# Grouped instance normalisation: VectorE alone normalises, with a shorter chain of statistics, fixed slots and half the instructions on VectorE and ScalarE

## The chip, the cores and the metric

One core of one Trainium2 chip. The metric is the device time of the whole program in microseconds (us), lower is better; most executions agree within 0.3%. With one core there is no second die to compare with; every run that is used here, unless the text says otherwise, was of the fast state, and the granted clock was 1.0 in all of them.

## The reference

```python
# x: (4, 8, 16, 256, 256) fp32, 134 MB;  gamma: (8, 16) fp32
mu  = x.mean(axis=(3, 4), keepdims=True)
var = ((x - mu) ** 2).mean(axis=(3, 4), keepdims=True)
out = (x - mu) / np.sqrt(var + 1e-5) * gamma[None, :, :, None, None]
```

512 channels of 65,536 numbers are each normalised on their own. All data is read once and written once: 134.2 MB in, 134.2 MB out.

## The kernel before

A unit is 16 channels, 128 partitions by 8,192 columns, 4 MB; there are 32 units and six buffers. All loads are issued by SyncE, all stores by ScalarE. A load waits until the store that empties its buffer has landed.

```python
    for u in range(6):
        load(u)                                   # nc.sync.dma_start, 4 MB each
    nc.scalar.dma_start(out=g_row[:], in_=gv[None, :])
    # ... gamma is spread to columns here, at the start: copy, 8 matmuls, copy

    def coefficients(u):                          # SQ = 4096
        nc.vector.reduce_sum(out=sums[:, j : j + 1], in_=t[:, a:b], axis=AX.X)
        for c in range(a, b, SQ):
            nc.scalar.activation(out=junk[:], in_=t[:, c : c + SQ], func=ACTF.Square,
                                 accum_out=sqs[:, n : n + 1])
        nc.vector.reduce_sum(out=mv[:, 0:1], in_=sums[:], axis=AX.X)
        nc.vector.reduce_sum(out=mv[:, 1:2], in_=sqs[:], axis=AX.X)
        nc.tensor.matmul(out=ps[:], lhsT=avg..., rhs=mv[:], start=True, stop=True)
        # then on VectorE: copy from PSUM, negate, variance; root on ScalarE;
        # reciprocal, times gamma, shift on VectorE
        ...
    for u in range(U):
        scale, shift = coefficients(u)
        norm_vector(t, 0, DV, scale, shift)       # DV = 5376 of 8192 columns
        norm_scalar(t, DV, F, scale, shift)       # the other 2816, on ScalarE
        nc.scalar.dma_start(out=ov[u], in_=t[:])
        if u + 6 < U:
            load(u + 6)
```

Of the kernel before, what the change touches and what calls it, by code (L numbers as in the profile page):

```python
# [6 lines left out]

F32 = mybir.dt.float32
BF16 = mybir.dt.bfloat16
ALU = mybir.AluOpType  # L10
ACTF = mybir.ActivationFunctionType
AX = mybir.AxisListType


@with_exitstack
def kernel(
    ctx: ExitStack,
    tc: tile.TileContext,
    x: bass.AP,
    gamma: bass.AP,  # L20
    out: bass.AP,
):
    nc = tc.nc
    B, G, C, H, W = x.shape
    P = nc.NUM_PARTITIONS
    HW = H * W
    n_ch = B * G * C
    S = 8
    K = P // S
    F = HW // S  # L30
    U = n_ch // K
    NG = (G * C) // K
    SQ = 4096
    DV = 5376
    assert HW % S == 0 and (G * C) % K == 0 and F % SQ == 0

    xv = x.rearrange("b g c h w -> (b g c h w)").rearrange("(u p f) -> u p f", p=P, f=F)
    ov = out.rearrange("b g c h w -> (b g c h w)").rearrange("(u p f) -> u p f", p=P, f=F)
    gv = gamma.rearrange("g c -> (g c)")

    data = ctx.enter_context(tc.tile_pool(name="data", bufs=6))
    singles = ctx.enter_context(tc.tile_pool(name="singles", bufs=1))
    stats_pool = ctx.enter_context(tc.tile_pool(name="stats", bufs=2))
    psum = ctx.enter_context(tc.tile_pool(name="psum", bufs=2, space=bass.MemoryType.PSUM))
    ctx.enter_context(tc.manual_schedule())

    def spans(widths):
        edges = [0]
        for w in widths:
            edges.append(edges[-1] + w)  # L50
        assert edges[-1] == F
        return list(zip(edges[:-1], edges[1:]))

    load_spans, store_spans = {}, {}
    whole = spans([F])

    tiles = {}

    def load(u):
        t = data.tile([P, F], F32, name="xt")  # L60
        for a, b in load_spans.get(u, whole):
            nc.sync.dma_start(out=t[:, a:b], in_=xv[u, :, a:b])
        tiles[u] = t

    for u in range(6):
        load(u)


    g_row = singles.tile([1, G * C], F32, name="g_row")
    nc.scalar.dma_start(out=g_row[:], in_=gv[None, :])  # L70
    eps_t = singles.tile([P, 1], F32, name="eps_t")
    nc.vector.memset(eps_t[:], 1e-5)
    avg = singles.tile([P, K, S], F32, name="avg")
    nc.gpsimd.memset(avg[:], 1.0 / HW)
    nc.gpsimd.affine_select(
        out=avg[:], in_=avg[:], pattern=[[-S, K], [0, S]], compare_op=ALU.is_ge,
        fill=0.0, base=0, channel_multiplier=1,
    )
    nc.gpsimd.affine_select(
        out=avg[:], in_=avg[:], pattern=[[S, K], [0, S]], compare_op=ALU.is_ge,  # L80
        fill=0.0, base=S - 1, channel_multiplier=-1,
    )
    one = singles.tile([1, 1], F32, name="one")
    nc.vector.memset(one[:], 1.0)
    g_rep = singles.tile([1, NG, K, S], F32, name="g_rep")
    nc.vector.tensor_copy(  # L86
        out=g_rep[:],
        in_=g_row[:].rearrange("o (n k) -> o n k", n=NG).unsqueeze(3).to_broadcast([1, NG, K, S]),
    )
    g_ps = psum.tile([P, NG], F32, name="g_ps", bufs=1)  # L90
    for n in range(NG):
        nc.tensor.matmul(  # L92
            out=g_ps[:, n : n + 1],
            lhsT=g_rep[:, n].rearrange("o k s -> o (k s)"),
            rhs=one[:],
            start=True, stop=True,
        )
    g_col = singles.tile([P, NG], F32, name="g_col")
    nc.vector.tensor_copy(out=g_col[:], in_=g_ps[:])  # L99

    junk = singles.tile([P, SQ], BF16, name="junk")

    def coefficients(u):
        t = tiles[u]
        sums = stats_pool.tile([P, len(load_spans.get(u, whole))], F32, name="sums")
        sqs = stats_pool.tile([P, F // SQ], F32, name="sqs")
        n = 0
        for j, (a, b) in enumerate(load_spans.get(u, whole)):
            nc.vector.reduce_sum(out=sums[:, j : j + 1], in_=t[:, a:b], axis=AX.X)  # L109
            for c in range(a, b, SQ):  # L110
                nc.scalar.activation(  # L111
                    out=junk[:], in_=t[:, c : c + SQ], func=ACTF.Square,
                    accum_out=sqs[:, n : n + 1],
                )
                n += 1
        mv = stats_pool.tile([P, 2], F32, name="mv")
        nc.vector.reduce_sum(out=mv[:, 0:1], in_=sums[:], axis=AX.X)  # L117
        nc.vector.reduce_sum(out=mv[:, 1:2], in_=sqs[:], axis=AX.X)  # L118
        ps = psum.tile([P, 2], F32, name="ps")
        nc.tensor.matmul(  # L120
            out=ps[:], lhsT=avg[:].rearrange("p k s -> p (k s)"), rhs=mv[:],
            start=True, stop=True,
        )
        cm = stats_pool.tile([P, 2], F32, name="cm")
        nc.vector.tensor_copy(out=cm[:], in_=ps[:])  # L125
        nmean = stats_pool.tile([P, 1], F32, name="nmean")
        nc.vector.tensor_scalar(  # L127
            out=nmean[:], in0=cm[:, 0:1], scalar1=-1.0, scalar2=None, op0=ALU.mult,
        )
        var = stats_pool.tile([P, 1], F32, name="var")  # L130
        nc.vector.scalar_tensor_tensor(  # L131
            out=var[:], in0=cm[:, 0:1], scalar=nmean[:], in1=cm[:, 1:2],
            op0=ALU.mult, op1=ALU.add,
        )
        std = stats_pool.tile([P, 1], F32, name="std")
        nc.scalar.activation(out=std[:], in_=var[:], func=ACTF.Sqrt, bias=eps_t[:], scale=1.0)  # L136
        rstd = stats_pool.tile([P, 1], F32, name="rstd")
        nc.vector.reciprocal(out=rstd[:], in_=std[:])  # L138
        scale = stats_pool.tile([P, 1], F32, name="scale")
        g = u % NG  # L140
        nc.vector.tensor_mul(out=scale[:], in0=rstd[:], in1=g_col[:, g : g + 1])  # L141
        shift = stats_pool.tile([P, 1], F32, name="shift")
        nc.vector.tensor_mul(out=shift[:], in0=nmean[:], in1=scale[:])  # L143
        return scale, shift

    def norm_vector(t, a, b, scale, shift):
        nc.vector.tensor_scalar(  # L147
            out=t[:, a:b], in0=t[:, a:b], scalar1=scale[:], scalar2=shift[:],
            op0=ALU.mult, op1=ALU.add,
        )  # L150

    def norm_scalar(t, a, b, scale, shift):
        nc.scalar.activation(  # L153
            out=t[:, a:b], in_=t[:, a:b], func=ACTF.Identity, bias=shift[:], scale=scale[:],
        )

    for u in range(U):
        scale, shift = coefficients(u)
        t = tiles.pop(u)
        if u in store_spans:  # L160
            for j, (a, b) in enumerate(store_spans[u]):
                (norm_scalar if j == 1 else norm_vector)(t, a, b, scale, shift)
            for a, b in store_spans[u]:
                nc.scalar.dma_start(out=ov[u, :, a:b], in_=t[:, a:b])
        else:
            norm_vector(t, 0, DV, scale, shift)
            norm_scalar(t, DV, F, scale, shift)
            nc.scalar.dma_start(out=ov[u], in_=t[:])
        if u + 6 < U:
            load(u + 6)  # L170


# [28 lines left out]
```

## Time and profile before

Before: 628.93 us (median of 3 runs, 628.9 to 629.06).

| | before |
|---|---|
| span of the profiled run | 627.1 us |
| moved | 268.5 MB at a mean of 428 GB/s |
| VectorE / ScalarE busy | 66% / 54% |
| a unit on the DMA engines | about 19.4 us for 4 MB in and 4 MB out |
| instructions in the profile | 937 |

From the page of the kernel before: the busy row of VectorE (DVE) and the DMA share in tenths over 40 equal slices of the span, the rate in each slice, and the DMA queues with their packets, megabytes and share of the 16 engines' time.

```profile
span 627.1 us, 937 instructions
...
DVE  2999657766577665686656866558665577655770
...
DMA  8999999999999999999999999999999999999997
GB/s 368 435 403 433 435 435 435 433 435 435 435 433 435 435 435 431 433 428 433 435 427 435 431 435 433 433 433 435 435 433 435 435 435 435 433 433 435 435 433 314
...
q1 hardware_dynamic: 4608, 134.22, 49.9%
q10 hardware_dynamic: 4610, 134.22, 49.6%
q14 instruction: 6, 0.05, 0.0%
...
```

The DMA engines are busy in all slices, at 427 to 435 GB/s nearly everywhere. Moving 268.4 MB at 435 GB/s takes 617.1 us, so only some 10 us of the span are open to any change. (The Trainium skill, "DMA: Bandwidth & Descriptors", Specifications, gives 435 GB/s as the ceiling of the fabric; the slices agree.)

The groups that matter, from the page of the kernel before (columns: line, engine, operation, out<-in, shapes, count, busy us, mean ns of one, then idle time before it and what ended it), and the DMA issues (KB, median us from issue to landing).

```profile
...
L109 DVE TENSOR_REDUCE sums<-xt 128x1 f32<-128x8192 f32 x32 | 277.9, 8686 | 150.4 <-DMA xt<-in_x_dram 150.4
...
L147 DVE TENSOR_SCALAR xt<-xt,scale,shift 128x5376 f32<-128x5376 f32 x32 | 98.5, 3079 | 1.2
L153 ACT ACTIVATE xt<-xt,shift,scale 128x2816 f32<-128x2816 f32 x32 | 87.5, 2734 | 22.0 <-DVE shift L143 22.0
...
out_dram<-xt ACTq DMA_DIRECT2D x32, 4096.0 KB, 41.3
...
```

VectorE's reduce waits 150 us in all for loads: the compute has slack in the middle of the run. Stores land 41 us after their issue, though 4 MB alone take under 10 us: both queues are several transfers deep.

The first store and the last unit, from the timeline of the kernel before (columns: start us, us, engine, line, operation).

```profile
...
27.46 0.38 ACTq L168 DMA_DIRECT2D out_dram<-xt  x1
...
```

```profile
...
598.43 8.69 DVE L109 TENSOR_REDUCE sums<-xt 128x1 f32<-128x8192 f32 x1 [5.13 <-DMA xt<-in_x_dram]
...
609.59 3.08 DVE L147 TENSOR_SCALAR xt<-xt,scale,shift 128x5376 f32<-128x5376 f32 x1
...
612.76 0.34 ACTq L168 DMA_DIRECT2D out_dram<-xt  x1
```

The first store is issued at 27.46. The last load has landed at 598.43; the last store is issued at 612.76, 14.33 us later. The tail, from a table of stretches (the last two columns are the share of the DMA engines and GB/s):

```profile
...
core 0: us, PE busy (x) PEld busy (x) DVE busy (x) ACT busy (x) POOL busy (x), PEclk, DMA share, GB/s
...
613.00:614.00 1.00, 0.00 (x0) 0.00 (x0) 0.00 (x0) 0.00 (x0) 0.00 (x0) 1.00 1.22 524
614.00:622.00 8.00, 0.00 (x0) 0.00 (x0) 0.00 (x0) 0.00 (x0) 0.00 (x0) 1.00 0.93 401
622.00:623.00 1.00, 0.00 (x0) 0.00 (x0) 0.00 (x0) 0.00 (x0) 0.00 (x0) 1.00 1.14 492
623.00:624.00 1.00, 0.00 (x0) 0.00 (x0) 0.00 (x0) 0.00 (x0) 0.00 (x0) 1.00 0.16 66
624.00:625.00 1.00, 0.00 (x0) 0.00 (x0) 0.00 (x0) 0.00 (x0) 0.00 (x0) 1.00 0.15 66
...
```

A finer table of the same stretch also has this line:

```profile
...
615.00:616.00 1.00, 0.00 (x0) 0.00 (x0) 0.00 (x0) 0.00 (x0) 0.00 (x0) 1.00 0.53 229
...
```

### The profile page before, as it was taken

What the parts mean: (1) busy time and instruction counts of PE and PEld (TensorE: products, weight loads), DVE (VectorE), ACT (ScalarE), POOL (GpSimd) and SP (SyncE); (2) the same over time, 40 slices, a digit from 0 to 9 for tenths busy, and PEclk for the clock granted to TensorE, in tenths of its full rate; (3) what the DMA queues carried; (4) which work ended last, traced back from release to release, by engine and by line L of the source; (5) the groups of instructions that cost most, each with busy time, mean ns of one, the idle gap of its engine ahead of it and who ended that gap; (6) DMA issues with size and microseconds to landing.
All of it is one profiled execution on the core that took longest, in us unless ns stands there. A gap on an engine that the chain in (4) does not pass through costs nothing.

```text
span 627.1 us, 937 instructions
## 1 busy us (share of the span) xinstructions
PE 22.3 (4%) x80; PEld 19.5 (3%) x80; DVE 416.5 (66%) x324; ACT 336.9 (54%) x194; POOL 1.2 (0%) x7
## 2 busy tenths in 40 slices
PE   2000000000000000000000000000000000000000
PEld 2000000000000000000000000000000000000000
DVE  2999657766577665686656866558665577655770
ACT  2877536555456464464634646446554455544560
POOL 0000000000000000000000000000000000000000
DMA  8999999999999999999999999999999999999997
GB/s 368 435 403 433 435 435 435 433 435 435 435 433 435 435 435 431 433 428 433 435 427 435 431 435 433 433 433 435 435 433 435 435 435 435 433 433 435 435 433 314
DMA packets 9224, 268.49 MB, mean 428 GB/s; under 512 B 1025, under 2 KB 1026, under 8 KB 1026
## 3 DMA queue, kind: packets, MB, share of 16 engines
q1 hardware_dynamic: 4608, 134.22, 49.9%
q10 hardware_dynamic: 4610, 134.22, 49.6%
q14 instruction: 6, 0.05, 0.0%
HBM read 134.22 MB, written 134.22 MB: 428 GB/s over the span
## 4 chain that ended last, share of the span: by engine, by line
DVE 67%; another core or an unknown queue 23%; PE 3%; DMA 2%; ACT 2%; issue 1%
DVE sums L109 44%; DVE xt L147 16%; PE ps L120 3%; DMA xt<-in_x_dram 2%; ACT std L136 2%; DVE var L131 1%; DVE rstd L138 1%; DVE cm L125 1%; DVE shift L143 1%; DVE scale L141 1%; DVE nmean L127 1%; DVE mv L117 1%; DVE mv L118 0%
## 5 line engine op out<-in xcount | busy, mean ns | idle before, releaser
L109 DVE TENSOR_REDUCE sums<-xt 128x1 f32<-128x8192 f32 x32 | 277.9, 8686 | 150.4 <-DMA xt<-in_x_dram 150.4
L111 ACT ACTIVATE junk<-xt 128x4096 bf16<-128x4096 f32 x64 | 231.5, 3617 | 166.8 <-DMA xt<-in_x_dram 163.5
L147 DVE TENSOR_SCALAR xt<-xt,scale,shift 128x5376 f32<-128x5376 f32 x32 | 98.5, 3079 | 1.2
L153 ACT ACTIVATE xt<-xt,shift,scale 128x2816 f32<-128x2816 f32 x32 | 87.5, 2734 | 22.0 <-DVE shift L143 22.0
L136 ACT ACTIVATE std<-var,eps_t 128x1 f32<-128x1 f32 x32 | 9.4, 294 | 85.4 <-DVE var L131 85.4
L120 PE MATMUL ps<-mv,avg 128*128 128x2 f32 x64 | 18.7, 362 | 582.9 <-DVE mv L118 582.9
L120 PEld LDWEIGHTS ps<-mv,avg 128*128 128x128 f32 x64 | 16.0, 311 | 585.6 <-DVE mv L118 569.8
L125 DVE COPY cm<-ps 128x2 f32<-128x2 f32 x32 | 5.1, 160 | 21.8 <-PE ps L120 21.8
L138 DVE RECIPROCAL rstd<-std 128x1 f32<-128x1 f32 x32 | 5.2, 164 | 11.6 <-ACT std L136 11.6
L111 ACT ACTIVATION_READ_ACCUMULATOR junk<-xt 128x1 f32 x64 | 11.9, 186 | 0.0
L131 DVE SCALAR_TENSOR_TENSOR var<-cm,nmean 128x1 f32<-128x1 f32 x32 | 7.0, 220 | 1.1
L143 DVE TENSOR_TENSOR shift<-nmean,scale 128x1 f32<-128x1 f32 x32 | 5.1, 159 | 1.1
L141 DVE TENSOR_TENSOR scale<-rstd,g_col 128x1 f32<-128x1 f32 x32 | 5.1, 159 | 1.1
L117 DVE TENSOR_REDUCE mv<-sums 128x1 f32<-128x1 f32 x32 | 4.9, 154 | 1.1
L127 DVE TENSOR_SCALAR nmean<-cm 128x1 f32<-128x1 f32 x32 | 4.9, 153 | 1.1
L118 DVE TENSOR_REDUCE mv<-sqs 128x1 f32<-128x2 f32 x32 | 4.7, 145 | 0.0
L92 PE MATMUL g_ps<-one,g_rep 1*128 1x1 f32 x16 | 3.6, 348 | 2.8 <-DVE g_rep L86 2.8
L92 PEld LDWEIGHTS g_ps<-one,g_rep 1*128 1x128 f32 x16 | 3.5, 325 | 2.8 <-DVE g_rep L86 2.8
L99 DVE COPY g_col<-g_ps 128x8 f32<-128x8 f32 x1 | 0.2, 167 | 3.7 <-PE g_ps L92 3.7
L111 ACT ACT_TABLE_LOAD x1 | 1.3, 1283 | 1.4 <-PEq L185 1.4
L86 DVE COPY g_rep<-g_row 1x1024 f32<-1x1024 f32 x1 | 0.7, 681 | 1.1 <-DMA g_row<-in_gamma_dram 1.1
L136 ACT ACT_TABLE_LOAD x1 | 1.3, 1283 | 0.0
(9 smaller groups left out, 1.5 us busy)
## 6 DMA issues: line engine op xcount, KB each, us to landing
xt<-in_x_dram SPq DMA_DIRECT2D x32, 4096.0 KB, 60.4
out_dram<-xt ACTq DMA_DIRECT2D x32, 4096.0 KB, 41.3
g_row<-in_gamma_dram ACTq DMA_DIRECT2D x1, 0.5 KB
```

The costliest lines, as they stand in the source:

```text
L109: nc.vector.reduce_sum(out=sums[:, j : j + 1], in_=t[:, a:b], axis=AX.X)
L111: nc.scalar.activation(out=junk[:], in_=t[:, c : c + SQ], func=ACTF.Square, accum_out=sqs[:, n : n + 1],)
L117: nc.vector.reduce_sum(out=mv[:, 0:1], in_=sums[:], axis=AX.X)
L120: nc.tensor.matmul(out=ps[:], lhsT=avg[:].rearrange("p k s -> p (k s)"), rhs=mv[:], start=True, stop=True,)
L125: nc.vector.tensor_copy(out=cm[:], in_=ps[:])
L131: nc.vector.scalar_tensor_tensor(out=var[:], in0=cm[:, 0:1], scalar=nmean[:], in1=cm[:, 1:2], op0=ALU.mult, op1=ALU.add,)
L136: nc.scalar.activation(out=std[:], in_=var[:], func=ACTF.Sqrt, bias=eps_t[:], scale=1.0)
L138: nc.vector.reciprocal(out=rstd[:], in_=std[:])
L141: nc.vector.tensor_mul(out=scale[:], in0=rstd[:], in1=g_col[:, g : g + 1])
L143: nc.vector.tensor_mul(out=shift[:], in0=nmean[:], in1=scale[:])
L147: nc.vector.tensor_scalar(out=t[:, a:b], in0=t[:, a:b], scalar1=scale[:], scalar2=shift[:], op0=ALU.mult, op1=ALU.add,)
L153: nc.scalar.activation(out=t[:, a:b], in_=t[:, a:b], func=ACTF.Identity, bias=shift[:], scale=scale[:],)
```

## The change

The intent: half the instructions on VectorE and ScalarE. The sum and the sum of squares go straight into the operand of the matmul, the variance is computed from PSUM in one operation, VectorE alone normalises (subtract the mean, read from PSUM as a scalar operand, then times scale), the buffers are six fixed slots and the statistics have a place of their own for each unit. The gamma columns are now made after the first unit's sums.

```diff
-    load_spans, store_spans = {}, {} ...            # six rotating tiles
+    slots = [data.tile([P, F], F32, name=f"xt{i}") for i in range(AHEAD)]
...
-    nc.scalar.dma_start(out=g_row[:], in_=gv[None, :])
+    for u in range(AHEAD):
+        load(u, nc.sync)
+        if u == 0:
+            nc.sync.dma_start(out=g_row[:], in_=gv[None, :])
...
+    for u in range(U):
+        nc.vector.reduce_sum(out=st[:, u, 0:1], in_=t[:], axis=AX.X)
+        nc.scalar.activation(out=junk[:], in_=t[:], func=ACTF.Square,
+                             accum_out=st[:, u, 1:2])          # 8192 columns at once
+        if u == 0:
+            gamma_columns()                          # was ahead of the loop
+        nc.tensor.matmul(out=ps[:], lhsT=navg_w, rhs=st[:, u], start=True, stop=True)
-        nc.vector.tensor_copy(out=cm[:], in_=ps[:])
-        ... negate, scalar_tensor_tensor ...
+        nc.vector.tensor_scalar(out=nvar..., in0=ps[:, 0:1], scalar1=ps[:, 0:1],
+                                scalar2=ps[:, 1:2], op0=ALU.mult, op1=ALU.add)
         ... root on ScalarE, reciprocal, times gamma ...
-        nc.vector.tensor_mul(out=shift[:], in0=nmean[:], in1=scale[:])
-            norm_vector(t, 0, DV, scale, shift)
-            norm_scalar(t, DV, F, scale, shift)
+        nc.vector.tensor_scalar(out=t[:], in0=t[:], scalar1=ps[:, 0:1],
+                                scalar2=scale[:, u : u + 1], op0=ALU.add, op1=ALU.mult)
         nc.scalar.dma_start(out=ov[u], in_=t[:])
```

More of the change, by code (lines that the diff above doesn't have):

```diff
@@ L8 @@
 F32 = mybir.dt.float32
-BF16 = mybir.dt.bfloat16
+U8 = mybir.dt.uint8
 ALU = mybir.AluOpType
@@ L32 @@
     NG = (G * C) // K
-    SQ = 4096
-    DV = 5376
-    assert HW % S == 0 and (G * C) % K == 0 and F % SQ == 0
+    AHEAD = 6
+    assert HW % S == 0 and (G * C) % K == 0
     xv = x.rearrange("b g c h w -> (b g c h w)").rearrange("(u p f) -> u p f", p=P, f=F)
@@ L39, with load @@
     gv = gamma.rearrange("g c -> (g c)")
-    data = ctx.enter_context(tc.tile_pool(name="data", bufs=6))
+    data = ctx.enter_context(tc.tile_pool(name="data", bufs=1))
     singles = ctx.enter_context(tc.tile_pool(name="singles", bufs=1))
-    stats_pool = ctx.enter_context(tc.tile_pool(name="stats", bufs=2))
-    psum = ctx.enter_context(tc.tile_pool(name="psum", bufs=2, space=bass.MemoryType.PSUM))
+    psum = ctx.enter_context(tc.tile_pool(name="psum", bufs=4, space=bass.MemoryType.PSUM))
     ctx.enter_context(tc.manual_schedule())
-    def spans(widths):
-        edges = [0]
-        for w in widths:
-            edges.append(edges[-1] + w)
-        assert edges[-1] == F
-        return list(zip(edges[:-1], edges[1:]))
-    load_spans, store_spans = {}, {}
-    whole = spans([F])
-    tiles = {}
-    def load(u):
-        t = data.tile([P, F], F32, name="xt")
-        for a, b in load_spans.get(u, whole):
-            nc.sync.dma_start(out=t[:, a:b], in_=xv[u, :, a:b])
-        tiles[u] = t
-    for u in range(6):
-        load(u)
+    slots = [data.tile([P, F], F32, name=f"xt{i}") for i in range(AHEAD)]
+    def load(u, queue):
+        queue.dma_start(out=slots[u % AHEAD][:], in_=xv[u])
     g_row = singles.tile([1, G * C], F32, name="g_row")
-    nc.scalar.dma_start(out=g_row[:], in_=gv[None, :])
+    for u in range(AHEAD):
+        load(u, nc.sync)
+        if u == 0:
+            nc.sync.dma_start(out=g_row[:], in_=gv[None, :])
     eps_t = singles.tile([P, 1], F32, name="eps_t")
-    nc.vector.memset(eps_t[:], 1e-5)
-    avg = singles.tile([P, K, S], F32, name="avg")
-    nc.gpsimd.memset(avg[:], 1.0 / HW)
+    nc.gpsimd.memset(eps_t[:], 1e-5)
+    one = singles.tile([1, 1], F32, name="one")
+    nc.gpsimd.memset(one[:], 1.0)
+    navg = singles.tile([P, K, S], F32, name="navg")
+    nc.gpsimd.memset(navg[:], -1.0 / HW)
     nc.gpsimd.affine_select(
-        out=avg[:], in_=avg[:], pattern=[[-S, K], [0, S]], compare_op=ALU.is_ge,
+        out=navg[:], in_=navg[:], pattern=[[-S, K], [0, S]], compare_op=ALU.is_ge,
         fill=0.0, base=0, channel_multiplier=1,
@@ L79 @@
     nc.gpsimd.affine_select(
-        out=avg[:], in_=avg[:], pattern=[[S, K], [0, S]], compare_op=ALU.is_ge,
+        out=navg[:], in_=navg[:], pattern=[[S, K], [0, S]], compare_op=ALU.is_ge,
         fill=0.0, base=S - 1, channel_multiplier=-1,
     )
-    one = singles.tile([1, 1], F32, name="one")
-    nc.vector.memset(one[:], 1.0)
+    navg_w = navg[:].rearrange("p k s -> p (k s)")
     g_rep = singles.tile([1, NG, K, S], F32, name="g_rep")
-    nc.vector.tensor_copy(
-        out=g_rep[:],
-        in_=g_row[:].rearrange("o (n k) -> o n k", n=NG).unsqueeze(3).to_broadcast([1, NG, K, S]),
-    )
@@ L90 @@
     g_ps = psum.tile([P, NG], F32, name="g_ps", bufs=1)
-    for n in range(NG):
-        nc.tensor.matmul(
-            out=g_ps[:, n : n + 1],
-            lhsT=g_rep[:, n].rearrange("o k s -> o (k s)"),
-            rhs=one[:],
-            start=True, stop=True,
-        )
-    g_col = singles.tile([P, NG], F32, name="g_col")
-    nc.vector.tensor_copy(out=g_col[:], in_=g_ps[:])
-    junk = singles.tile([P, SQ], BF16, name="junk")
-    def coefficients(u):
-        t = tiles[u]
-        sums = stats_pool.tile([P, len(load_spans.get(u, whole))], F32, name="sums")
-        sqs = stats_pool.tile([P, F // SQ], F32, name="sqs")
-        n = 0
-        for j, (a, b) in enumerate(load_spans.get(u, whole)):
-            nc.vector.reduce_sum(out=sums[:, j : j + 1], in_=t[:, a:b], axis=AX.X)
-            for c in range(a, b, SQ):
-                nc.scalar.activation(
-                    out=junk[:], in_=t[:, c : c + SQ], func=ACTF.Square,
-                    accum_out=sqs[:, n : n + 1],
-                )
-                n += 1
-        mv = stats_pool.tile([P, 2], F32, name="mv")
-        nc.vector.reduce_sum(out=mv[:, 0:1], in_=sums[:], axis=AX.X)
-        nc.vector.reduce_sum(out=mv[:, 1:2], in_=sqs[:], axis=AX.X)
@@ new lines, with gamma_columns @@
+    g_col = singles.tile([P, NG], F32, name="g_col")
+    def gamma_columns():
+        nc.vector.tensor_copy(
+            out=g_rep[:],
+            in_=g_row[:].rearrange("o (n k) -> o n k", n=NG).unsqueeze(3).to_broadcast([1, NG, K, S]),
+        )
+        for n in range(NG):
+            nc.tensor.matmul(
+                out=g_ps[:, n : n + 1],
+                lhsT=g_rep[:, n].rearrange("o k s -> o (k s)"),
+                rhs=one[:],
+                start=True, stop=True,
+            )
+        nc.vector.tensor_copy(out=g_col[:], in_=g_ps[:])
@@ new lines @@
+    junk = singles.tile([P, F], U8, name="junk")
+    st = singles.tile([P, U, 2], F32, name="st")
+    nvar = singles.tile([P, U], F32, name="nvar")
+    std = singles.tile([P, U], F32, name="std")
+    rstd = singles.tile([P, U], F32, name="rstd")
+    scale = singles.tile([P, U], F32, name="scale")
+    squares = []
+    for u in range(U):
+        t = slots[u % AHEAD]
+        nc.vector.reduce_sum(out=st[:, u, 0:1], in_=t[:], axis=AX.X)
+        square = nc.scalar.activation(
+            out=junk[:], in_=t[:], func=ACTF.Square, accum_out=st[:, u, 1:2],
+        )
+        if u:
+            tc.declare_no_dep(square.ins, squares[-1].ins, reason="junk, ordered by the root between")
+        squares.append(square)
+        if u == 0:
+            gamma_columns()
@@ L119, in coefficients @@
         ps = psum.tile([P, 2], F32, name="ps")
-        nc.tensor.matmul(
-            out=ps[:], lhsT=avg[:].rearrange("p k s -> p (k s)"), rhs=mv[:],
-            start=True, stop=True,
-        )
-        cm = stats_pool.tile([P, 2], F32, name="cm")
-        nc.vector.tensor_copy(out=cm[:], in_=ps[:])
-        nmean = stats_pool.tile([P, 1], F32, name="nmean")
+        nc.tensor.matmul(out=ps[:], lhsT=navg_w, rhs=st[:, u], start=True, stop=True)
+        nc.vector.tensor_scalar(
+            out=nvar[:, u : u + 1], in0=ps[:, 0:1], scalar1=ps[:, 0:1],
+            scalar2=ps[:, 1:2], op0=ALU.mult, op1=ALU.add,
+        )
@@ L127, in coefficients @@
+        nc.scalar.activation(
+            out=std[:, u : u + 1], in_=nvar[:, u : u + 1], func=ACTF.Sqrt,
+            bias=eps_t[:], scale=-1.0,
+        )
+        nc.vector.reciprocal(out=rstd[:, u : u + 1], in_=std[:, u : u + 1])
+        g = u % NG
+        nc.vector.tensor_mul(
+            out=scale[:, u : u + 1], in0=rstd[:, u : u + 1], in1=g_col[:, g : g + 1],
+        )
         nc.vector.tensor_scalar(
-            out=nmean[:], in0=cm[:, 0:1], scalar1=-1.0, scalar2=None, op0=ALU.mult,
-        )
@@ L130, in coefficients @@
-        var = stats_pool.tile([P, 1], F32, name="var")
-        nc.vector.scalar_tensor_tensor(
-            out=var[:], in0=cm[:, 0:1], scalar=nmean[:], in1=cm[:, 1:2],
-            op0=ALU.mult, op1=ALU.add,
-        )
-        std = stats_pool.tile([P, 1], F32, name="std")
-        nc.scalar.activation(out=std[:], in_=var[:], func=ACTF.Sqrt, bias=eps_t[:], scale=1.0)
-        rstd = stats_pool.tile([P, 1], F32, name="rstd")
-        nc.vector.reciprocal(out=rstd[:], in_=std[:])
-        scale = stats_pool.tile([P, 1], F32, name="scale")
@@ L140, in coefficients @@
-        g = u % NG
-        nc.vector.tensor_mul(out=scale[:], in0=rstd[:], in1=g_col[:, g : g + 1])
-        shift = stats_pool.tile([P, 1], F32, name="shift")
-        nc.vector.tensor_mul(out=shift[:], in0=nmean[:], in1=scale[:])
-        return scale, shift
-    def norm_vector(t, a, b, scale, shift):
-        nc.vector.tensor_scalar(
-            out=t[:, a:b], in0=t[:, a:b], scalar1=scale[:], scalar2=shift[:],
-            op0=ALU.mult, op1=ALU.add,
-        )
-    def norm_scalar(t, a, b, scale, shift):
-        nc.scalar.activation(
-            out=t[:, a:b], in_=t[:, a:b], func=ACTF.Identity, bias=shift[:], scale=scale[:],
-        )
@@ L157 @@
-    for u in range(U):
-        scale, shift = coefficients(u)
-        t = tiles.pop(u)
-        if u in store_spans:
-            for j, (a, b) in enumerate(store_spans[u]):
-                (norm_scalar if j == 1 else norm_vector)(t, a, b, scale, shift)
-            for a, b in store_spans[u]:
-                nc.scalar.dma_start(out=ov[u, :, a:b], in_=t[:, a:b])
-        else:
-            norm_vector(t, 0, DV, scale, shift)
-            norm_scalar(t, DV, F, scale, shift)
-            nc.scalar.dma_start(out=ov[u], in_=t[:])
-        if u + 6 < U:
-            load(u + 6)
+            out=t[:], in0=t[:], scalar1=ps[:, 0:1], scalar2=scale[:, u : u + 1],
@@ L174 @@
+            op0=ALU.add, op1=ALU.mult,
+        )
+        nc.scalar.dma_start(out=ov[u], in_=t[:])
+        if u + AHEAD < U:
+            load(u + AHEAD, nc.sync)
 _INS = ['x', 'gamma']
```

## The prediction

> **What bounds it now.** The DMA engines. The slice table shows DMA share 9 in 38 of 40 slices at 427 to 435 GB/s; the queue table shows 268.5 MB moved. 268.4 MB / 435 GB/s = 617.1 us of a 627.1 us span. (The Trainium skill, "DMA: Bandwidth & Descriptors", Specifications, calls 435 GB/s the SBUF fabric ceiling; the trace agrees.) The remaining 10 us: about 1.5 us before data flows, 2.4 us from last byte (about 624.7) to end (receipt), about 1 us idle before the last store, the rest the ramp and a slow stretch (360 GB/s) at 27 to 35 us. VectorE is 66% and ScalarE 54% busy; in the waits, VectorE's reduce idles 150 us for loads: compute is off the path except at the ends.
>
> **What the change does, per unit** (timeline of the last unit: load landed 598.43, store issued 612.76, 14.33 us):
> - Reduce's end (607.11) to normalisation's start (609.59) is 2.48 us; two tiny reduces, the PSUM copy, negation and shift go. New chain: reduce, matmul (0.62), one op from PSUM (about 0.2), root 0.29, reciprocal and product 0.16 each, hand-overs 0.2: estimate 1.65 us, 0.8 saved.
> - VectorE normalises 8192 instead of 5376 columns. 3079 ns for 5376 is 0.52 ns an element plus about 280 ns, so the estimate for 8192 is 4.55 us, +1.47. This assumes that the two-elements-per-cycle mode survives a per-partition scalar in PSUM. The skill ("VectorE: DVE Perf Modes", perf-mode tier table) caps tensor inputs from PSUM for fp32 at one per cycle; I take a scalar operand not to count. If it does, the op takes about 8.7 us.
> - Store issue therefore 15.0 us after landing, 0.65 us later. VectorE about 15 us a unit, against the 19.35 us that DMA needs. ScalarE falls to about 7.7 us a unit.
> - Gamma: its columns are now made after the first reduce (copy 0.68, sixteen PE passes 3.5, copy 0.17): first store issued at about 32.3 us, not 27.5.
>
> **The critical path.** Loads run alone until the first store; then both queues are always backlogged (stores land 41 us after issue, loads 60) and share equally. So the lead that loads have when the first store is issued, 2.6 units before, persists to the end: 2.6 units x 9.65 us = 25 us of stores left when the last load lands at 598.4, which gives 623.5; the trace's last byte is at 624.7. Without the last unit that is 15.5 us, barely the 14.3 us of compute plus latency: hence 1 us idle. After, the later first store makes the lead about 3.1 units: the last load lands about 4 to 5 us earlier (about 594), 20 us of stores then hide the 15.0 us of compute. The idle vanishes; the slower unit costs nothing; gain about 1 us.
>
> **Prediction: 628.0 us**, 8 in 10 between 626.8 and 630.5. Faster by over 2%: 0.01; within: 0.94; slower: 0.05.
>
> **What would show it.** DMA share 9 throughout, 433 to 435 GB/s; the normalisation 4.5 to 4.6 us; first store near 32 us; last load landing 593 to 596; last store issued before its predecessor has drained; VectorE about 77% busy, ScalarE about 40%; instructions about 550.
>
> **What would make it wrong.** The normalisation at 8.7 us: VectorE then needs about 19.1 us a unit, no slack beside DMA's 19.35, and the end moves to 633 to 642. Or the lead does not persist: then the 0.65 us longer unit shows at the end, 629.5. Or the slow stretch where stores begin changes length.

## The result, and the profile after

After: 627.19 us (median of 4 runs, 627.09 to 627.37); before, in the same rounds, 628.99 us (4 runs, 628.9 to 629.29). Ratio 0.9971, 95% interval 0.9954 to 0.9988: a gain of 0.3%, under the 2% that counts as faster, but clear of the noise. A ratio is the mean time of one kernel's fast runs over that of the other's of the same rounds, so not quite the ratio of the medians that are quoted.

The page of the changed kernel, the same lines:

```profile
span 625.2 us, 626 instructions
...
DVE  1699999786666867668776677666786766867660
...
DMA  8999999999999999999999999999999999999998
GB/s 369 436 409 430 436 436 436 436 436 436 430 436 430 430 424 434 436 436 434 436 436 434 432 436 428 430 428 434 436 436 434 436 436 434 432 434 430 428 430 367
...
q14 instruction: 2, 0.02, 0.0%
...
```

The DMA rows look the same; the instruction packets are two instead of six. The groups and issues:

```profile
...
L101 DVE TENSOR_REDUCE st<-xt 128x1 f32<-128x8192 f32 x32 | 277.9, 8684 | 119.7 <-DMA xt<-in_x_dram 119.7
...
L126 DVE TENSOR_SCALAR xt<-xt,ps,scale 128x8192 f32<-128x8192 f32 x32 | 145.6, 4550 | 1.2
...
out_dram<-xt ACTq DMA_DIRECT2D x32, 4096.0 KB, 52.6
...
```

The normalisation of 8,192 columns takes 4,550 ns, as estimated: a scalar operand in PSUM does not cost the higher rate (with two tensor inputs, in e5, the same work took 8,757 ns). The Trainium skill ("VectorE: DVE Perf Modes", under the perf-mode tier table) caps an fp32 operation with "any PSUM operand" at one element per cycle; here a tensor in SBUF with its scalar in PSUM is not capped.

The first store and the last unit, from the timeline of the changed kernel:

```profile
...
22.43 3.54 PE L82 MATMUL g_ps<-one,g_rep 1*128 1x1 f32 x16 [22.43 <-DVE g_rep L77]
...
26.90 1.28 ACT L117 ACT_TABLE_LOAD   x1 [6.77 <-DVE nvar L113]
...
33.50 0.37 ACTq L130 DMA_DIRECT2D out_dram<-xt  x1
...
```

```profile
...
590.27 8.69 DVE L101 TENSOR_REDUCE st<-xt 128x1 f32<-128x8192 f32 x1 [4.35 <-DMA xt<-in_x_dram]
...
600.74 4.55 DVE L126 TENSOR_SCALAR xt<-xt,ps,scale 128x8192 f32<-128x8192 f32 x1
605.32 0.34 ACTq L130 DMA_DIRECT2D out_dram<-xt  x1
```

The first store is issued at 33.50, 6.0 us later than before: besides the gamma columns and the longer normalisation, the load of the root's table (1.28 us), which before lay under VectorE's reduce, now lies open. The last load has landed at 590.27, and the last store is issued at 605.32, 15.05 us later. The tail of the changed kernel:

```profile
...
622.00:623.00 1.00, 0.00 (x0) 0.00 (x0) 0.00 (x0) 0.00 (x0) 0.00 (x0) 1.00 0.38 164
623.00:624.00 1.00, 0.00 (x0) 0.00 (x0) 0.00 (x0) 0.00 (x0) 0.00 (x0) 1.00 0.01 0
...
```

From 623 on nothing is left, where before two or three engines had two more microseconds to do.

### Where the 1.8 us came from

The trace holds more than these views print: the start and length of each DMA packet, and the time of each of the 16 part-completions of every DMA (one from each DMA engine). I worked two things out from these records.

First, the idle that I had read into the last store is not there. Counting the packets in flight, 15.2 to 16.0 of 16 engines are busy from 610 to 622.5 us in the kernel before; the dip at 613 to 614 is worth 0.04 us of the whole.

Second, the engines do not finish together. In the last store of the kernel before, the median of the 16 part-completions came at 623.84 us and the last at 626.15, 2.31 us late; the next two were 1.90 and 0.86 late. After, the median came at 623.47 and the last 0.65 late. So of 2.03 us in these two profiles, 1.66 us is the latest engine, and 0.37 us is common to all engines. (The spans of the two profiles differ by 1.9 us, the medians of the timed runs by 1.8.)

The lateness grows in steps through the run, and each step coincides with one of the 8 KB packets on the instruction queue. Such a packet is called a fetch here: I take it to bring the next instructions of one engine, which e3 and e4 test. Lateness of the three latest engines against the median of 16, in us, in the last transfer landed ahead of such a packet, and in one that landed over 20 us after it (worked out from the part-completions):

```
kernel before    fetch at  78.60:  0.18 0.18 0.24  ->  0.12 0.18 0.72
                 fetch at 117.41:  0.15 0.17 0.74  ->  0.10 0.43 0.63
                 fetch at 321.47:  0.40 0.40 0.60  ->  0.38 0.50 1.55
                 fetch at 399.93:  0.35 0.62 1.49  ->  0.69 1.00 1.46
                 fetch at 505.63:  0.87 0.92 1.43  ->  0.86 1.41 1.67
                 fetch at 554.71:  0.88 1.43 1.67  ->  0.88 1.77 2.39
changed kernel   fetch at 158.24:  0.15 0.31 0.32  ->  0.26 0.29 0.84
                 fetch at 222.33:  0.22 0.27 0.81  ->  0.24 0.42 0.74
```

Right behind each of them, one data packet took 0.25 to 0.58 us longer than the usual 1.213 us, and the fetch itself took 0.309 us. The engines have no idle time in which such a loss could be made good, so most of it stays until the end (0.74 us at 90 us is still 0.60 at 306). Not all lateness is steps: in the kernel before, the third latest engine goes from 0.10 us at 148 us to 0.40 at 306, with no fetch between; no run shows why.

This gives two theories. **L (lead)** is the one that I predicted: the later first store gives loads a longer lead, so that the last unit's compute is hidden. **F (fetch)**: programs of fewer instructions are fetched in fewer blocks; each fetch holds up one DMA engine by 0.56 to 0.89 us (the 0.309 us and the 0.25 to 0.58 us from above), and the kernel ends with the engine that was held up most. A third, **U (unit chain)**, is the plain one: what counts is how long a unit takes on VectorE.

### The profile page after: what moved, and what is told of

Read it like the earlier page. It is cut to its first block, busy times and chain, and to the rows that moved or that the text cites. A ratio compares the mean times of both kernels' runs of the same rounds, so it can differ in the third digit from the quotient of the medians.

```text
span 625.2 us, 626 instructions
## 1 busy us (share of the span) xinstructions
PE 21.3 (3%) x80; PEld 19.5 (3%) x80; DVE 443.2 (71%) x162; ACT 239.9 (38%) x98; POOL 1.3 (0%) x9
## 4 chain that ended last, share of the span: by engine, by line
DMA 76%; DVE 18%; PE 2%; issue 0%; ACT 0%; SPq 0%; ACTq 0%
DMA xt<-in_x_dram 72%; DVE st L101 15%; DMA out_dram<-xt 5%; DVE xt L126 2%; PE ps L112 1%; PE g_ps L82 1%; DVE nvar L113 0%; ACT L117 0%; ACT std L117 0%; DVE g_rep L77 0%; DVE rstd L121 0%; DVE scale L123 0%; SPq L48 0%; ACTq L117 0%
## 5 line engine op out<-in xcount | busy, mean ns | idle before, releaser
L101 DVE TENSOR_REDUCE st<-xt 128x1 f32<-128x8192 f32 x32 | 277.9, 8684 | 119.7 <-DMA xt<-in_x_dram 119.7
L102 ACT ACTIVATE junk<-xt 128x8192 uint8<-128x8192 f32 x32 | 224.9, 7030 | 275.3 <-DMA xt<-in_x_dram 242.9
L126 DVE TENSOR_SCALAR xt<-xt,ps,scale 128x8192 f32<-128x8192 f32 x32 | 145.6, 4550 | 1.2
L117 ACT ACTIVATE std<-nvar,eps_t 128x1 f32<-128x1 f32 x32 | 9.4, 294 | 77.6 <-DVE nvar L113 77.6
L112 PE MATMUL ps<-st,navg 128*128 128x2 f32 x64 | 17.9, 349 | 555.9 <-DVE st L101 555.9
L112 PEld LDWEIGHTS ps<-st,navg 128*128 128x128 f32 x64 | 16.0, 311 | 557.7 <-issue 557.6
L113 DVE TENSOR_SCALAR nvar<-ps 128x1 f32<-128x1 f32 x32 | 9.2, 287 | 23.4 <-PE ps L112 23.4
L102 ACT ACTIVATION_READ_ACCUMULATOR junk<-xt 128x1 f32 x32 | 6.0, 186 | 0.0
```

What stands on the lines that cost most here:

```text
L101: nc.vector.reduce_sum(out=st[:, u, 0:1], in_=t[:], axis=AX.X)
L102: square = nc.scalar.activation(out=junk[:], in_=t[:], func=ACTF.Square, accum_out=st[:, u, 1:2],)
L112: nc.tensor.matmul(out=ps[:], lhsT=navg_w, rhs=st[:, u], start=True, stop=True)
L113: nc.vector.tensor_scalar(out=nvar[:, u : u + 1], in0=ps[:, 0:1], scalar1=ps[:, 0:1], scalar2=ps[:, 1:2], op0=ALU.mult, op1=ALU.add,)
L117: nc.scalar.activation(out=std[:, u : u + 1], in_=nvar[:, u : u + 1], func=ACTF.Sqrt, bias=eps_t[:], scale=-1.0,)
L126: nc.vector.tensor_scalar(out=t[:], in0=t[:], scalar1=ps[:, 0:1], scalar2=scale[:, u : u + 1], op0=ALU.add, op1=ALU.mult,)
```

## The experiments

Twelve runs, all with correct results.

### e1: the kernel before, gamma columns after the first sums

```diff
+        if u == 0:
+            gamma_columns()       # moved from ahead of the loop
         ps = psum.tile([P, 2], F32, name="ps")
```

> The kernel before, with one thing changed: the gamma columns are made after the first unit's sums instead of at the start, so the first store is issued at about 33 us instead of 27.5, as in the changed kernel. Theory L (the lead of loads over stores, as I predicted: a later first store hides the last unit and ends the idle before the last store): about 627.2, at least 1 us faster than before. Theory F (instruction fetches: six 8 KB fetches during the run of before against two after, each holding up one DMA engine by 0.6 to 0.9 us, so that the engine that is hit most often drains last): unchanged, 628.7 to 629.2, six fetches on the instruction queue as in before.

Measured: 629.05 us (628.66 to 629.63) against 628.88 for the kernel before, ratio 1.0003 (0.9989 to 1.0016); first store issued at 31.49 us; six fetches. L's gain of 1 us is not there. In its profile the median engine was done at 623.28, 0.56 us earlier than before, but the latest engine was 3.66 us late, more than three fetches explain: a data packet at 113.3 us took 0.8 us longer than usual with no fetch beside it (the next fetch is at 114.5), and one at 93.6 us took 0.35 us longer. With these two, the sum for VectorE's three fetches (2.53 us, worked out as under e7) becomes 3.68. So this run is not a clean measure; e12 repeats the test.

### e2: the kernel before with the short statistics

```diff
-        sums, sqs, two small reduces, copy from PSUM, negate, ...
+        nc.vector.reduce_sum(out=mv[:, 0:1], in_=t[:], axis=AX.X)
+        nc.scalar.activation(out=junk[:], in_=t[:], func=ACTF.Square, accum_out=mv[:, 1:2])
+        ... matmul, variance from PSUM in one operation, as in the changed kernel
```

> The kernel before with the short chain of statistics of the changed kernel (one square, no copy from PSUM, no negation, single reduce), so about a third fewer instructions; the split normalisation, the early gamma columns, the rotating tiles and the early first store (about 26.7 us) stay. F: two or three fetches on the instruction queue, and 627.2 to 627.9. L: the first store is as early as before, so no gain by more than 0.3 us: 628.6 to 629.0.

Measured: 628.49 us (628.01 to 628.62), ratio 0.9991 (0.9979 to 1.0004). The number of fetches was mis-estimated: five, not two or three, since ScalarE, which still normalises its part, kept most of its instructions (130 of 194 in the profile). The latest engine was 1.46 us late instead of 2.31. The lateness agrees with F's sense, half of F's number is missed, and the gain in time is not clear of noise: suggestive only.

### e3: the changed kernel with 640 idle memsets on GpSimd

```diff
+    for _ in range(640):
+        nc.gpsimd.memset(pad[:], 0.0)
```

> The changed kernel with 640 small memsets added on GpSimd, which is otherwise idle and which nothing waits for; no wait and no operation of the other engines changes. F: four or five more fetches on the instruction queue in the first 80 us or so, all by one engine; if fetches of one issuing engine go over the same DMA engine, that one drains 3 to 4 us late: 629.4 to 630.6; if they spread over DMA engines, 627.2 to 628. L and any theory of the compute chain: 627.2.

Measured: 629.24 us (628.91 to 629.88), 2.1 us above the changed kernel, with no operation of another engine touched; seven fetches, five of them between 11 and 118 us while GpSimd ran. The instruction line of its page:

```profile
...
q14 instruction: 7, 0.06, 0.0%
...
```

The latest engine was 2.64 us late. It is slightly below my range for one and the same DMA engine: five fetches gave 2.6 us and not 3 to 4. The packets show most of the reason: right behind GpSimd's fetches the data packet took 0.22 to 0.35 us longer than usual, behind VectorE's in e4 0.43 to 0.61. With the 0.309 us of each fetch that sums to 3.01 us. Why the last 0.4 us of it are missing is open. Neither L nor U has any room for this result.

### e4: the changed kernel with ten memsets a unit on VectorE

```diff
         nc.scalar.dma_start(out=ov[u], in_=t[:])
+        for _ in range(10):
+            nc.vector.memset(pad[:], 0.0)
```

> The changed kernel with ten memsets of one column added on VectorE after each unit's normalisation (320 in all, about 1 us a unit, VectorE still has over 3 us of slack a unit). F: two or three more fetches, 628.5 to 629.7. L and any theory of the compute chain: 627.2 (the store of the unit is not delayed, and the last unit's chain is the same).

Measured: 629.90 us (629.68 to 630.06), 0.2 us above my range, with three fetches more than the changed kernel. The instruction line of its page, and its tail as a table of stretches:

```profile
...
q14 instruction: 5, 0.04, 0.0%
...
```

```profile
...
622.00:623.00 1.00, 0.00 (x0) 0.00 (x0) 0.00 (x0) 0.00 (x0) 0.00 (x0) 1.00 0.46 197
623.00:624.00 1.00, 0.00 (x0) 0.00 (x0) 0.00 (x0) 0.00 (x0) 0.00 (x0) 1.00 0.01 0
624.00:625.00 1.00, 0.00 (x0) 0.00 (x0) 0.00 (x0) 0.00 (x0) 0.00 (x0) 1.00 0.08 33
625.00:626.00 1.00, 0.00 (x0) 0.00 (x0) 0.00 (x0) 0.00 (x0) 0.00 (x0) 1.00 0.08 33
626.00:627.00 1.00, 0.00 (x0) 0.00 (x0) 0.00 (x0) 0.00 (x0) 0.00 (x0) 1.00 0.00 0
...
```

From 624 to 626 us a share of 0.08, about one engine of 16, is still draining. The part-completions give the steps of the latest engine: 0.15 to 0.99 at the fetch at 70 us, 0.95 to 1.88 at 220 us, 1.74 to 2.73 at 379 us, 2.70 to 3.47 at 553 us. At these four times VectorE had started 50, 184, 305 and 439 instructions, so they are taken to be VectorE's (8 KB is 128 instructions, an estimate by the size in the Trainium skill, "Runtime: NRT & Kernel Launch", Instruction fetch mechanics, which counts 256 to 16 KiB). The records do not name the DMA engine, but only the largest lateness rose at all four, by 0.77 to 0.99 us each, so they fell on the same one. The fifth, at 222 us, comes when ScalarE has started 61 instructions, as in the changed kernel, and hit another engine.

### e5: the changed kernel with a normalisation of half the rate

```diff
-        nc.vector.tensor_scalar(out=t[:], in0=t[:], scalar1=ps[:, 0:1],
-            scalar2=scale[:, u : u + 1], op0=ALU.add, op1=ALU.mult)
+        nc.vector.scalar_tensor_tensor(out=t[:], in0=t[:], scalar=ps[:, 0:1],
+            in1=scale[:, u : u + 1].to_broadcast([P, F]), op0=ALU.add, op1=ALU.mult)
```

> The changed kernel with the normalisation written as an operation with two tensor inputs (the scale broadcast), same instruction count, same result, about 8.7 us instead of 4.55: the unit's chain is 4 us longer and VectorE needs about 19.0 us a unit beside the 19.36 us that DMA needs. Theory U (the length of a unit's chain, or VectorE's load, is in the time): at least 4 us slower than the changed kernel, 631 or more. Theory F (only the DMA engine that drains last counts, and two fetches as before the edit): 627.0 to 628.0, since the trace of the changed kernel has the last store issued about 8 us before its turn.

Measured: 645.13 us (645.06 to 645.23), ratio 1.0258 (1.0244 to 1.0271). Here U is right, and what I had expected from F was wrong. From its page (rates, and the two groups), and its last stores in the timeline of ScalarE's queue:

```profile
...
GB/s 375 440 393 442 424 432 442 430 424 440 438 424 434 440 428 428 440 434 426 438 438 426 430 440 434 426 436 440 428 428 440 434 426 438 438 428 430 238 261 261
...
L101 DVE TENSOR_REDUCE st<-xt 128x1 f32<-128x8192 f32 x32 | 277.8, 8680 | 13.0 <-DMA xt<-in_x_dram 13.0
L126 DVE SCALAR_TENSOR_TENSOR xt<-xt,ps,scale 128x8192 f32<-128x8192 f32 x32 | 280.2, 8757 | 1.1
...
```

```profile
...
611.85 0.34 ACTq L131 DMA_DIRECT2D out_dram<-xt  x1
...
630.99 0.34 ACTq L131 DMA_DIRECT2D out_dram<-xt  x1
```

The operation takes 8,757 ns, and VectorE waited for a load only once, for the first (13.0 us). VectorE is now the bound: stores are issued every 19.14 us (630.99 less 611.85), from about 37.7 on (630.99 less 31 times 19.14). That is faster than the 19.36 us that DMA needs for a unit, and I took that for slack. But VectorE starts a unit late and has no time to catch up before the last turn comes, at about 613 us. So the DMA engines run dry: the last slices show 238 to 261 GB/s. By this account a unit may cost VectorE about 18.5 us ((613 less 38) over 31), not 19.36: an estimate that no run tests.

### e6: the changed kernel with one VectorE instruction a unit less

```diff
-            ... func=ACTF.Sqrt ...
-        nc.vector.reciprocal(out=rstd[:, u : u + 1], in_=std[:, u : u + 1])
+            ... func=ACTF.Abs_reciprocal_sqrt ...
```

> The changed kernel with one VectorE instruction a unit taken out (ScalarE gives the reciprocal root directly), about 132 instead of 164 instructions on VectorE; ScalarE's count is the same. F: one or two fetches; if VectorE's own fetch goes, the slowest DMA engine is 0.4 us late instead of 0.65: 626.7 to 627.2. A change of this size may not be resolved. The reciprocal root may be less exact; the result decides whether it passes.

Measured: 627.35 us (627.19 to 627.7), ratio 0.9976 (0.9964 to 0.9988), correct. Still two fetches, VectorE's only later (197 us instead of 158); the latest engine was 0.87 us late. No gain, and no fetch was saved: the run does not test F.

### e7: the padding of e4, split over two engines

```diff
+        for _ in range(5):
+            nc.vector.memset(pad[:], 0.0)
+            nc.scalar.activation(out=pad_s[:], in_=eps_t[:], func=ACTF.Square)
```

> The changed kernel with five small memsets a unit on VectorE and five small activations a unit on ScalarE, after the store is issued: as many added instructions as in the run with ten memsets on VectorE (which had five fetches, four of them VectorE's, and took 629.9), but split over two issuing engines. F in the form that each issuing engine's fetches go over one DMA engine, so that the largest count of one issuing engine decides: five or six fetches, at most three by one engine, the last store 2.3 to 2.6 us late on one DMA engine: 628.6 to 629.2, so faster than the run with ten on VectorE. F in the form that the total of fetches decides: 629.9 to 630.6.

Measured: 628.92 us (628.68 to 628.93). The instruction line of its page:

```profile
...
q14 instruction: 6, 0.05, 0.0%
...
```

Six fetches, one more than in e4, and yet 1 us faster than e4. The latest engine was 2.38 us late. So it is not the total of fetches that counts but what falls on one DMA engine. The lateness is that of three fetches, as expected if the fetches of one issuing engine add up on one DMA engine.

The packets give this sum directly: for each fetch 0.309 us, and what the data packet right behind it took over 1.213 us. VectorE's four in e4 make 3.36 us (latest engine 3.37), its three here 2.40 (2.38), its three in the kernel before 2.58 (2.31), its one in the changed kernel 0.84 (0.65). ScalarE's three here make only 1.57, and the second latest engine was 1.43 late. So fetches differ in cost, and their number alone does not decide.

### e8 and e10: the changed kernel with early gamma columns, twice

```diff
-            nc.sync.dma_start(out=g_row[:], in_=gv[None, :])
+            nc.scalar.dma_start(out=g_row[:], in_=gv[None, :])
-        if u == 0:
-            gamma_columns()
+    gamma_columns()               # ahead of the loop
```

> The changed kernel with the gamma columns made before the first unit's sums and gamma loaded on the other queue, as in the kernel before: the first store is issued at about 29 us instead of 33.5. L as I predicted (the lead hides the last unit): the last store would still be issued in time at this lead, or up to 1 us would come back: 627.2 to 628.2. F: two fetches, and no change but what the moment at which stores begin costs (13 of 16 engines ended 0.4 us earlier in runs whose first store was issued after 31 us): 627.1 to 627.7.

> The changed kernel with early gamma columns once more, unchanged from the run that took 631 to 663 with data packets of 1.21 us drawn out to 1.23 to 1.27 on average. If that was the kernel itself (the moment of the first store, 29.45 us): slow again, above 630. If it came from that chip or that loading of the program: 627.1 to 627.7, packets at 1.213 us.

Measured: 650.11 us (631.16 to 662.88) and, on another chip, 654.50 us (648.78 to 671.22), six runs each; the kernel before, run in turn with them, stayed between 628.7 and 629.9. These runs scatter so widely that several count as slow against the fastest of their own kernel; by those that count as fast the ratios are 1.0107 (1.0052 to 1.0162) and 1.0364 (1.033 to 1.0398). Neither theory had expected this, and the repeat shows that it belongs to the kernel. The page of the repeat's profiled run, which counts as fast among its own:

```profile
span 647.1 us, 626 instructions
...
GB/s 387 423 411 423 409 415 421 429 433 423 420 425 425 419 426 425 429 417 438 417 421 427 413 436 417 417 427 417 427 413 429 419 425 429 425 423 423 405 302 275
...
```

The rate is 405 to 438 GB/s between the first slice and the last two, and 415 in the mean; in the last two it falls to 302 and 275: the last unit's load lands at 616.92 and its store is issued at 631.98, when the other stores have all but drained. Before that the engines are not idle, but slower: between 60 and 560 us some 650 data packets took over 1.3 us, where the changed kernel has two; the mean packet took 1.24 us instead of 1.213.

### e11: early gamma columns, first store held back

```diff
+        if u == 0:
+            nc.vector.reduce_sum(out=spare[:], in_=t[:, 0:3840], axis=AX.X)
         nc.vector.tensor_scalar(out=t[:], in0=t[:], ...
```

> Early gamma columns, and the first unit's normalisation held back by one extra reduce of 3840 columns (about 4.15 us), so that the first store is issued at about 33.6 us as in the changed kernel. If the moment of the first store made the slow run, this one is 627.1 to 627.4; if the early gamma code did it in another way, it is slow too; if it was the chip, both this and the repeat are fast.

Measured: 626.95 us (626.91 to 627.06), ratio 0.9967 (0.9955 to 0.9979). One useless instruction of 4.14 us made the kernel about 25 us faster (e10's fast runs have a mean of 651.96). The first stores of e10 and of e11, from their timelines, and e11's page:

```profile
...
29.37 0.38 ACTq L129 DMA_DIRECT2D out_dram<-xt  x1
...
```

```profile
...
33.48 0.38 ACTq L132 DMA_DIRECT2D out_dram<-xt  x1
...
```

```profile
span 625.3 us, 627 instructions
...
GB/s 371 434 415 432 428 436 436 436 436 436 434 436 432 430 428 430 430 434 436 436 436 436 434 436 434 430 430 430 428 436 434 436 436 436 436 434 432 434 428 354
...
```

So the moment of the first store decides. What it sets is the lead of loads over stores, worked out at 300 us from the packets: 3.14 units in e8 (whose profile counts as slow) and in e10; 2.75 and 2.84 in e2 and the kernel before; 3.35 to 3.91 in all others. At leads on both sides packets take 1.213 us. That the lead is the cause is not shown: up to 170 us e1 had a lead of 3.14 to 3.22, and apart from those behind fetches only two packets, at 93.6 and 113.3 us, were drawn out. Why the moment is bad no run shows.

### e9: the changed kernel again

No edit.

> The changed kernel as it is, again, as the measure for the others of this call: 627.0 to 627.5, two fetches.

Measured: 627.12 us (626.99 to 627.25), ratio 0.9969 (0.9957 to 0.9981), two fetches.

### e12: the kernel before, first store held back

```diff
+            if u == 0:
+                nc.vector.reduce_sum(out=spare[:], in_=t[:, 0:F], axis=AX.X)
             norm_vector(t, 0, DV, scale, shift)
```

> The kernel before with one extra instruction: a reduce over the first unit on VectorE ahead of its normalisation, 8.7 us, so that the first store is issued at about 36 us instead of 27.5. L as I predicted: 627.2, at least 1 us faster. F: six fetches as before, the slowest DMA engine 2.3 us late; the small part of lateness that all engines share (0.4 us, seen with first stores after 31 us) may go: 628.4 to 629.0.

Measured: 628.71 us (628.53 to 629.45) against 629.02, ratio 0.9997 (0.9984 to 1.001); first store issued at 36.16 us, six fetches. The median engine was done at 623.47, exactly as in the changed kernel and 0.37 us earlier than before; the latest was 2.52 us late. So a later first store is worth 0.3 to 0.4 us by the trace, too little to be resolved in time. L's 627.2 is refuted; a gain of just 1 us lies at the edge of this interval, and outside e1's.

The packets also show where the 0.3 to 0.4 us lie. Between 20 and 60 us, where stores begin, packets are drawn out by 1.03 us per DMA engine in the kernel before and 1.02 in e2, whose first stores are early, and by 0.54 to 0.78 in the runs of the table below that start storing after 31 us. The moment alone does not set it: e5, with its first store at 37.65, has 1.16. What does, no run shows.

### All runs in one table

Fetches are those during the run; "median" and "late" are of the 16 part-completions of the last DMA to land in the profiled run.

| run | fetches | first store issued | median, us | late, us | time, median us |
|---|---|---|---|---|---|
| before | 6 | 27.46 | 623.84 | 2.31 | 628.99 |
| after | 2 | 33.50 | 623.47 | 0.65 | 627.19 |
| e9 after again | 2 | 33.55 | 623.38 | 0.69 | 627.12 |
| e2 before, short statistics | 5 | 27.08 | 623.84 | 1.46 | 628.49 |
| e1 before, gamma late | 6 | 31.49 | 623.28 | 3.66 | 629.05 |
| e12 before, first store late | 6 | 36.16 | 623.47 | 2.52 | 628.71 |
| e3 after, GpSimd padded | 7 | 33.87 | 623.49 | 2.64 | 629.24 |
| e4 after, VectorE padded | 5 | 33.48 | 623.53 | 3.37 | 629.90 |
| e7 after, padding split | 6 | 33.45 | 623.55 | 2.38 | 628.92 |
| e6 after, one instruction less | 2 | 33.34 | 623.48 | 0.87 | 627.35 |
| e11 early gamma, store late | 2 | 33.48 | 623.40 | 0.81 | 626.95 |

e5, e8 and e10 are left out: VectorE, or drawn-out packets, set their time. Median plus late, plus about 3 us of end, gives the time of each row within 0.3 us; only e1, which scattered by 1 us and whose profile fell on its slowest run (629.63), is 0.9 us off. No version beats the changed kernel clearly: e11 is 0.17 us faster than e9, with the intervals of their ratios overlapping. What F leaves to gain is the 0.65 us of lateness, 0.1% of the time.

## Why the prediction was right or wrong, point by point

- **Time.** 627.19 us lies within 626.8 to 630.5, and within 2%, as predicted. The forecast gain was about 1 us, the measured one 1.8 us. That the number came so close is in part luck: the term that was to give the gain was not there, and another, which was not in the sum, gave most of it.
- **"The DMA engines" bound it.** Right. In e5 alone VectorE took their place.
- **"About 1 us idle before the last store".** Wrong, and this is the step that failed. It was read from bins of 1 us whose shares ran from 0.53 to 1.22; the packets show 0.04 us. The last byte, read from such bins as landing at about 624.7, landed at 626.15, so the late engines were overlooked. With it falls "the idle vanishes ... gain about 1 us". In its place: three DMA engines ended up to 2.3 us after the rest, and after the change the latest only by 0.65. That the fetches of instructions cause most of the lateness is shown by the steps in the trace, by e3 and e4, which bring the lateness back with operations that nothing waits for, and by e7. What a later first store is worth is 0.37 us (e12), and not by ending an idle time: packets are less drawn out where stores begin (0.76 us per DMA engine in e12, 1.03 before). The prediction had named that stretch, but only as a risk.
- **Instructions.** I listed "instructions about 550" (they went from 937 to 626; on VectorE from 324 to 162, on ScalarE from 194 to 98) as a by-product and gave it no cost, though the instruction queue stood in the profile's table of queues. This was the term that was missing from the sum, worth 1.66 us of 2.03 in the profiles.
- **The unit's chain.** Right: 4.55 us for the normalisation (4,550 ns), 15.0 us from landing to store (15.05), and the longer chain costs nothing: the last store is issued at 605.32, and the packets show that its data starts to move at 613.2.
- **The lead persists.** Right in kind: at 300 us 2.84 units before and 3.39 after (2.6 and 3.1 predicted). First store: 32.3 predicted, 33.50 measured, since I forgot the table load (1.28 us) that the new order lays open. Last load landed: about 594 predicted, 590.27 measured.
- **VectorE "about 77% busy".** 71%: hand-overs between engines are not busy time. ScalarE 38%, predicted 40%.
- **The risk that I named.** If the normalisation took 8.7 us, 633 to 642 was predicted; e5 took 645.1 with 8.76 us. The direction was right and the size too small; the expectation that I wrote for e5 itself (627 to 628) was plainly wrong, since I compared 19.1 us with 19.36 and forgot that VectorE has to make up its late start.
- **Left open.** Why a first store at 29.4 us draws out the packets; the slow growth of lateness between fetches; the two drawn-out packets of e1; why the data packet behind a fetch is held up longer for VectorE than for ScalarE or GpSimd.

## What to carry to other kernels

When a kernel is bound by DMA, look at when each of the DMA engines finishes, not at their mean share: 0.99 of 16 engines can hide one that is 2 us late. Instructions off every critical path still cost there, because their fetches run over the same DMA engines; what counts is the largest sum of hold-ups on one DMA engine. So shorten first the instruction stream whose fetches add up to most, and by enough to save a fetch: 32 instructions less on VectorE saved none in e6. And the moment of the first store fixes the lead of loads over stores for the whole run: try a few, because one of them cost 3.6% here, and a change that seems to gain may only have moved away from it.

## What the Trainium skill lacked or had wrong

- "Runtime: NRT & Kernel Launch", Instruction fetch mechanics, says that crossing a block's boundary costs "one DMA tail-bump, mostly hidden". For the DMA engine that serves it, each fetch cost 0.77 to 0.99 us (VectorE's four in e4), and in this DMA-bound kernel this is in the time: 629.90 against 627.12 us. The page also gives 16 KiB blocks; the trace shows one packet of 8,192 bytes at a time, at intervals of 121 to 134 VectorE instructions.
- No page says that the fetches of one issuing engine fall on one and the same DMA engine, as e4 (four, 3.37 us late) and e7 (six in all, 2.38 us late) indicate.
- "Perfetto Trace Analysis", Identifying the Most-Contended Engine, rightly calls the occupancy of DMA misleading because there are 16 engines, and puts HBM utilisation in its place. That doesn't show the late engine either: the mean rate was 428 GB/s before and 429 after. The page goes on to name single DMA engines among what can bind, but not that one of them can end late (2.31 us here) while the mean is full.
- "VectorE: DVE Perf Modes", perf-mode tier table: neither its "any-PSUM" column nor the "any PSUM operand" of the text below it says whether a scalar operand counts. It does not: 4,550 ns for 8,192 fp32 columns with the mean in PSUM, against 8,757 ns for the form with two tensor inputs.
- "DMA: Bandwidth & Descriptors" has nothing on a rate that depends on when writes start beside reads; here a first store at 29.37 us (e10) gave 415 GB/s, and one at 33.48 us (e11) gave 429.
